# An encoder block on one core: the first pass's loads through one queue, and its side work over more ticks

## The chip, the cores and the metric

The kernel runs on one core of one Trainium2 chip. The metric is the device time of one execution in microseconds (us), lower is better. The kernel before the change takes 3470.04 us (median of 3 runs, 3468.87 to 3470.82).

## The reference

512 tokens of width 2048 in float32 go through one block. What matters here:

```python
h = rms_norm(x, norm1_g);  proj = h @ w_in           # 2048 x 8200: q, k, v, forget logits, pool input, gates
q, k = rms_norm over each head's 128 columns         # 8 heads
attn = softmax(q k' / sqrt(128) + (c_q - c_k), causal) v      # c = cumsum(log_sigmoid(forget logits))
y_attn = attn @ w_branch_attn;  y_pool = multiscale_pool(pin) @ w_branch_pool
x = x + (sig(g_A)*y_attn + sig(g_B)*y_pool) @ w_out
xn = rms_norm(x, norm2_g);  query = xn @ peer_w_query
# per token and head: top 16 of 128 scores twice, top 16 of their 256 sums, softmax,
# then 16 rows of expert_u and of expert_v (16384 x 2048 each)
x = x + sum over heads and picks of gelu(u . xn) * gate * v
```

## The kernel before

The tokens are split in three. The first 128 ("A") go through a **first pass** of their own (about 0 to 436 us); their expert rows are then gathered one by one beside the later passes. The other 384 ("B") go through the same projections in a second run over the weights, and 320 of them meet all experts as dense products. The change touches the first pass alone.

**Weights.** The first pass reads 112 weight tiles of 128 x 2048 float32 (1 MB each): 64 of `w1A` (16 groups of 512 columns, four tiles per group), then 16 each of `wbrA`, `woA` and `wquA`. SP issues every tile's load, in order, as soon as a raw buffer is free (`ensure_load`, L148): three `wraw` buffers and, until the last group of `wbrA`, one `xraw`. Of `w1A`, `wbrA` and `woA` every third tile is used raw, as float32; the other two of three are split in two halves: ScalarE rounds a half to `whi` (L162), VectorE forms the rest, `wlo` (L174). Of `wquA` two of three are raw. A raw buffer is free again when TensorE has read the raw tile, or when `wlo` of the second half is done.

**TensorE's tile** is `mmA` (L240): four steps of K = 128 into 128 x 512 of PSUM, one matmul per step for a raw tile and three for a split one.

**Order.** All engines take their instructions in program order, and the program is written as a schedule by hand. Side work stands in Python generators. In the middle of each weight tile (`kk == 1`) one **tick** runs: every live generator emits what it has up to its next `yield`. `next_w` (L186) emits splits for the tile at hand and the next before the tile's matmuls, `ahead` (L194) emits one more `whi` after them, `after` (L198) the matching `wlo`. `run_gens_last` runs a new generator's first piece at once, between `ahead` and `after`.

**What is touched, in the order of time:**
- Start (L275 to L282): `xA` (the A tokens, transposed, four pieces of 256 KB) and `xr0` (the same tokens as rows, 1 MB) are issued by ScalarE, the first three weight tiles by SP. Then, for each of four pieces (L349 to L352): VectorE multiplies by `g1`, ScalarE rounds, VectorE subtracts; the first weight tile's split stands behind the first piece. Behind all four stands L358, ScalarE's sum of squares of `xr0`, which gives `rsn`, the rows' norm (`narrow_rstd`, emitted in the first tile). `wpg` (1 MB, needed by the pooling generators) is issued by ScalarE at L364.
- Head norms (`qkA_norm`, L475): per group of q or k one eviction (L383), four sums of squares (L480), one Ln and one Exp on ScalarE between VectorE's steps (L482, L321 to L325), a multiply, and three ticks later the transposes. `attendA` (L498) waits five ticks from the v group's end, then uses them; its four `ck` rows (L505) are issued by SP.
- Rows of the other tokens (`rest_rstd`, L545): three 1 MB loads `row<-x` by SP, beside the weights.
- Second inputs (`inputs_b`, L642): sixteen K steps of the B tokens, loaded in pairs by POOL (`xB`, eight loads of 384 KB, two buffers), each multiplied by VectorE (L656), rounded by ScalarE (L658), and its rest formed by VectorE (L662) one or two ticks later.
- Second norm of A (`normedA`, L672), and the scores with top-k (`scores_a`, L866; `job`, L725).

Of the kernel before, what the change touches and what calls it, by code (L numbers as in the profile page):

```python
# [12 lines left out]
F32 = mybir.dt.float32  # L13
# [4 lines left out]
AF = mybir.ActivationFunctionType  # L18
OP = mybir.AluOpType
# [43 lines left out]
def block_kernel(ctx, tc, a):  # L63
# [211 lines left out]
    g1 = const.tile([P, KD], F32, name="g1")  # L275
    nc.gpsimd.dma_start(g1, a["g1"])
    for c in range(4):
        nc.scalar.dma_start(xA[:, 4 * c:4 * c + 4, :].rearrange("p k t -> p (k t)"),
                            a["xA"][:, 4 * c * NA:4 * (c + 1) * NA])
    ensure_load(0)  # L280
    nc.scalar.dma_start(xr0, a["x"][0:P])
    ensure_load(2)  # L282
    jp = const.tile([P, P], I32, name="jp")
    nc.gpsimd.iota(jp, pattern=[[1, P]], base=0, channel_multiplier=-1)
    iot = const.tile([P, P], F32, name="iot")
# [69 lines left out]
            ensure_split(1)  # L355
    nc.vector.tensor_scalar(qg, qg, float(np.float32(P ** -0.5)), None, op0=OP.mult)
    sq0 = row_tile()
    nc.scalar.activation(sq0, xr0, AF.Square, accum_out=ssn[:, 0:1])  # L358
    zA = pz.tile([P, 2 * D], F32, name="zA")
    ap32 = pz.tile([P, KD, NA], F32, name="ap32")  # L360
    aph = pA.tile([P, KD, NA], F32R, name="YH")
    apl = pA.tile([P, KD, NA], F32R, name="YL")
    wpgA = p1.tile([P, D], F32, name="wpg")
    nc.scalar.dma_start(wpgA, a["wpg"])  # L364

    bands = p1.tile([P, 4, P], F32, name="bands")
    bt = p1.tile([P, P], F32, name="bt")
# [106 lines left out]

    def qkA_norm(which, hb, ps):  # L475
        t = rowsA(ps, "raw", 3)
        v = p1.tile([P, 12], F32, name="hv", bufs=2)
        sq = p1.tile([P, S], F32, name="sqA")
        for j in range(4):
            nc.scalar.activation(sq[:, j * P:(j + 1) * P], t[:, j * P:(j + 1) * P], AF.Square,  # L480
                                 accum_out=v[:, j:j + 1])
        nc.vector.tensor_scalar(v[:, :4], v[:, :4], 1.0 / P, EPS, op0=OP.mult, op1=OP.add)  # L482
        rsqrt_nr(v[:, 4:8], v[:, :4], v[:, 8:])
        yield
        nc.vector.tensor_tensor(quad(t), quad(t), v[:, 4:8, None].to_broadcast([P, 4, P]), op=OP.mult)
        for _ in range(3):
            yield
        pt = bank()
        for j in range(4):
            nc.tensor.transpose(pt[:, j * P:(j + 1) * P], t[:, j * P:(j + 1) * P], ident)  # L490
        out = p1.tile([P, 4, NA], F32, name="n%d" % which)
        nc.scalar.activation(out.rearrange("p j t -> p (j t)"), pt, AF.Copy,
                             scale=(kg if which else qg)[:, 0:1])
        qkA[which, hb] = out
        if which:
            nc.scalar.dma_start(kA_d[hb], out)

    def attendA(hb, ps):  # L498
        vA = p1.tile([P, 4, P], F32, name="vA")
        nc.scalar.activation(vA.rearrange("p j t -> p (j t)"), ps, AF.Copy, scale=rsn[:, 0:1])  # L500
        nc.scalar.dma_start(vA_d[hb], vA)
        ck = p1.tile([P, 4, NA], F32, name="ck")
        for j in range(4):
            h = 4 * hb + j
            nc.sync.dma_start(ck[:, j, :], c_d[h:h + 1, :NA].to_broadcast([P, NA]))  # L505
        for _ in range(5):
            yield
        qn, kn = qkA.pop((0, hb)), qkA.pop((1, hb))
        pss = bank()
        for j in range(4):  # L510
            nc.tensor.matmul(pss[:, j * P:(j + 1) * P], lhsT=qn[:, j, :], rhs=kn[:, j, :],
                             start=True, stop=True)
        pr = p1.tile([P, 4, NA], F32, name="prA")
        sm = p1.tile([P, 4, 2], F32, name="smA", bufs=2)
        for j in range(4):
            h = 4 * hb + j
            nc.vector.scalar_tensor_tensor(pr[:, j, :], ck[:, j, :], cT[:, 0, h:h + 1],
                                           pss[:, j * P:(j + 1) * P], op0=OP.subtract, op1=OP.subtract)
        nc.vector.tensor_tensor(pr, pr, mask[:, None, :].to_broadcast([P, 4, NA]), op=OP.add)
        nc.vector.tensor_reduce(sm[:, :, 0:1], pr, axis=AX.X, op=OP.min)  # L520
        yield
        for j in range(4):
            nc.scalar.activation(pr[:, j, :], pr[:, j, :], AF.Exp, bias=sm[:, j, 0:1], scale=-1.0,
                                 accum_out=sm[:, j, 1:2])
        yield
        nc.vector.reciprocal(sm[:, :, 1:2], sm[:, :, 1:2])
        nc.vector.tensor_tensor(pr, pr, sm[:, :, 1:2].to_broadcast([P, 4, NA]), op=OP.mult)
        yield
        yield
        yield  # L530
        pt = bank()
        for j in range(4):
            nc.tensor.transpose(pt[:, j * P:(j + 1) * P], pr[:, j, :], ident)
        PT = p1.tile([P, 4, NA], F32, name="PT")
        nc.scalar.copy(PT.rearrange("p j t -> p (j t)"), pt)
        yield
        yield
        pa = bank()
        for j in range(4):
            nc.tensor.matmul(pa[:, j * P:(j + 1) * P], lhsT=vA[:, j, :], rhs=PT[:, j, :],  # L540
                             start=True, stop=True)
        nc.scalar.copy(ap32[:, 4 * hb:4 * hb + 4, :].rearrange("p j t -> p (j t)"), pa)
        split_to(ap32, aph, apl, 4 * hb)
# [14 lines left out]
    for n, (kind, i) in enumerate(groups_a):  # L558
        ps = acc_bank()
        for q in range(4):  # L560
            mmA(ps, xA, hAh, hAl, 4 * q, q == 0, q == 3, run_gens)
            if n == 0 and q == 0:
                narrow_rstd(0, 1)
            ahead()
            if q < 3:
                after()
        if kind == "pin":
            gens.append(poolA(i, ps))
            if i == 1:
# [72 lines left out]
    def inputs_b():  # L642
        rb = row_bcast(p2, [rsn[:, b:b + 1] for b in range(1, NTB)], "rstdB")
        xs = {}

        def load(c):
            xs[c] = p2.tile([P, 2, NB], F32, name="xB", bufs=2)
            nc.gpsimd.dma_start(xs[c].rearrange("p j t -> p (j t)"), a["xB"][c])

        load(0)  # L650
        for c in range(KD // 2):
            if c + 1 < KD // 2:
                load(c + 1)
            for j in range(2):
                k = 2 * c + j
                nc.vector.scalar_tensor_tensor(xs[c][:, j, :], xs[c][:, j, :], g1[:, k:k + 1], rb,  # L656
                                               op0=OP.mult, op1=OP.mult)
                nc.scalar.copy(hh[:, k, :], xs[c][:, j, :])  # L658
                yield
                if j:  # L660
                    yield
                nc.vector.tensor_tensor(hl[:, k, :], xs[c][:, j, :], hh[:, k, :].bitcast(F32),  # L662
                                        op=OP.subtract)

    gens.append(inputs_b())
    nAh = pA.tile([P, KD, NA], F32R, name="YH")
# [5 lines left out]
    def normedA(i):  # L672
# [5 lines left out]
        for j in range(4):  # L678
            nc.tensor.transpose(tb[:, j * P:(j + 1) * P], xs[:, j * P:(j + 1) * P], ident)
        nc.vector.tensor_tensor(n32[:, 4 * i:4 * i + 4, :], quad(tb),  # L680
                                g2[:, 4 * i:4 * i + 4, None].to_broadcast([P, 4, NA]), op=OP.mult)
        split_to(n32, nAh, nAl, 4 * i)
        yield
        t = p3.tile([P, S], F32, name="scr", bufs=2)
# [181 lines left out]
    def scores_a(c, ps, kk):  # L866
# [18 lines left out]
        scored.append(c)  # L885
        for j in range(2):
            yield from blkA.job(2 * c + j, (s[:, 2 * j, :], s[:, 2 * j + 1, :]))
        chosen.append(c)

    scored, chosen = [], []  # L890
# [706 lines left out]
```

## Time and profile before

| | |
|---|---|
| median of 3 runs | 3470.04 us |
| the profiled execution | 3467.64 us, its span 3465.8 us |
| TensorE matmul busy | 3334.0 us, 96% |
| VectorE / ScalarE / GpSimd busy | 2685.1 us (77%) / 1515.4 us (44%) / 652.4 us (19%) |
| HBM | 980.05 MB read, 53.56 MB written, 298 GB/s over the span |

Engines: PE is TensorE's matmul, PEld its weight load, DVE VectorE, ACT ScalarE, POOL GpSimd, SP SyncE; ACTq, SPq and POOLq are their sequencers, which issue DMAs. Times in the rows are microseconds from the span's start; busy time is the union of an engine's instructions in a stretch. A wait is named by what ended it: `PE psm L240 <- DVE wlo L174` means that the matmul of line 240 began when VectorE's instruction of line 174, which writes `wlo`, had ended. "PEclk" is the clock that TensorE was granted, as a share of 2.4 GHz; 0.50 is 1.2 GHz.

### The profile page before, as it was taken

The page shows a single profiled execution, that of the slowest core. Times are in us where ns is not written, and L with a number is a line of the kernel's source. Part 1 is how long each engine was busy: PE and PEld are TensorE (multiplying, and loading weights), DVE is VectorE, ACT ScalarE, POOL GpSimd, SP SyncE. Part 2 cuts the span into 40 slices and gives each one's busy share as a digit, 9 for nine tenths or more (in the row PEclk, how much of TensorE's full clock was granted, in tenths as well). Part 3 has the DMA queues.
Part 4 walks back from the last instruction along what each step waited for, and adds up shares of the span by engine and source line. Part 5 has one row for each costly group of instructions (what it writes and reads, how often), then busy time and mean ns, then how long its engine had stood idle before and what let it go on. Part 6 is the DMA issues. An engine that isn't in the chain of part 4 may idle for free.

```text
span 3465.8 us, 50471 instructions
## 1 busy us (share of the span) xinstructions
PE 3334.0 (96%) x20236; PEld 3155.4 (91%) x20236; DVE 2685.1 (77%) x3482; ACT 1515.4 (44%) x2263; POOL 652.4 (19%) x411
## 2 busy tenths in 40 slices
PE   7999899999998999999999989999999999999998
PEld 5656599999998999999999989999999999999997
DVE  5556787787876876887778758888887888888885
ACT  5655434545443333346476753333333333333332
POOL 0000012233321221310000002222222222222221
PEclk9999999999998999999999999999999999999999
DMA  7898867787877897864555689999998999899994
GB/s 263 305 360 313 312 239 272 268 312 268 309 288 283 319 362 278 312 229 161 201 189 193 215 305 345 357 355 351 350 347 338 359 354 354 338 358 353 340 357 151
DMA packets 226762, 1036.90 MB, mean 299 GB/s; under 512 B 21344, under 2 KB 107536, under 8 KB 112928
## 3 DMA queue, kind: packets, MB, share of 16 engines
q1 hardware_dynamic: 144640, 574.14, 44.4%
q0 software_dynamic: 56480, 406.96, 31.5%
q10 hardware_dynamic: 25408, 52.59, 3.9%
q8 instruction: 158, 2.59, 0.3%
q14 instruction: 76, 0.62, 0.0%
HBM read 980.05 MB, written 53.56 MB: 298 GB/s over the span
## 4 chain that ended last, share of the span: by engine, by line
PE 55%; DVE 14%; issue 12%; DMA 8%; ACT 7%; POOL 2%; ACTq 0%; SPq 0%; POOLq 0%; DVEq 0%
PE psm L223 9%; PE psm L221 9%; PE psm L222 9%; PE psv L222 6%; PE psv L223 6%; PE psv L221 6%; PE psm L240 6%; DVE wlo L174 5%; DMA row<-v,gidx 3%; ACT whi L162 3%; ACT o L1385 2%; DVE tok L827 1%; POOL row L787 1%; PE psx L222 1%; PE psx L223 1%
## 5 line engine op out<-in xcount | busy, mean ns | idle before, releaser
L174 DVE TENSOR_TENSOR wlo<-wraw,whi 128x1024 fp32r<-128x1024 f32 x728 | 869.2, 1220 | 294.9 <-ACT whi L162 291.6
L162 ACT CAST whi<-wraw 128x1024 fp32r<-128x1024 f32 x728 | 753.5, 1047 | 658.0 <-PE psv L222 375.9
L223 PE MATMUL psv<-h5h,wlo 128*128 128x320 f32 x2048 | 636.1, 311 | 14.3 <-DVE wlo L174 14.3
L221 PE MATMUL psm<-xnh,whi 128*128 128x320 f32 x2048 | 637.4, 311 | 10.3 <-ACT at L1410 9.8
L221 PE MATMUL psv<-h5h,whi 128*128 128x320 f32 x2048 | 636.7, 311 | 6.6 <-ACT h5h L1442 6.4
L223 PE MATMUL psm<-xnh,wlo 128*128 128x320 f32 x2048 | 634.3, 310 | 6.7 <-DVE wlo L174 6.6
L222 PE MATMUL psv<-h5l,whi 128*128 128x320 f32 x2048 | 637.4, 311 | 1.1
L222 PE MATMUL psm<-xnl,whi 128*128 128x320 f32 x2048 | 633.8, 309 | 0.0
L787 POOL DMA_INDIRECT row<-v,gidx x139 | 219.1, 1576 | 1136.4 <-DVE tok L827 1090.1
L223 PEld LDWEIGHTS psv<-h5h,wlo 128*128 128x128 f32 x2048 | 386.9, 189 | 15.3 <-DVE wlo L174 15.3
L221 PEld LDWEIGHTS psm<-xnh,whi 128*128 128x128 f32 x2048 | 386.5, 189 | 10.8 <-ACT at L1410 10.0
L221 PEld LDWEIGHTS psv<-h5h,whi 128*128 128x128 f32 x2048 | 387.0, 189 | 8.8 <-ACT h5h L1442 8.8
L223 PEld LDWEIGHTS psm<-xnh,wlo 128*128 128x128 f32 x2048 | 386.3, 189 | 8.1 <-DVE wlo L174 8.1
L222 PEld LDWEIGHTS psv<-h5l,whi 128*128 128x128 f32 x2048 | 386.9, 189 | 4.9 <-DVE h5l L1443 4.6
L222 PEld LDWEIGHTS psm<-xnl,whi 128*128 128x128 f32 x2048 | 386.5, 189 | 0.0
L221 PE MATMUL psm<-hh,whi 128*128 128x384 f32 x1024 | 353.6, 345 | 0.0
L787 POOL DMA_INDIRECT row<-u,gidx x135 | 223.8, 1658 | 660.1 <-DVE row L824 567.2
L222 PE MATMUL psm<-hl,whi 128*128 128x384 f32 x1024 | 346.4, 338 | 0.0
L223 PE MATMUL psm<-hh,wlo 128*128 128x384 f32 x1024 | 346.4, 338 | 0.0
L827 DVE SCALAR_TENSOR_TENSOR tok<-row,gact,tok 128x2048 f32<-128x2048 f32 x139 | 326.0, 2345 | 19.1 <-DMA row<-v,gidx 18.0
L824 DVE SCALAR_TENSOR_TENSOR row<-row,tok 128x2048 f32<-128x2048 f32 x135 | 307.4, 2284 | 9.1 <-DMA row<-u,gidx 9.0
L162 ACT CAST whi<-xraw 128x1024 fp32r<-128x1024 f32 x148 | 153.5, 1046 | 182.2 <-PE psv L222 145.7
(393 smaller groups left out, 5183.4 us busy)
## 6 DMA issues: line engine op xcount, KB each, us to landing
wraw<-uT SPq DMA_DIRECT2D x112, 1024.0 KB, 6.7
wraw<-vd SPq DMA_DIRECT2D x96, 1024.0 KB, 7.4
wraw<-w1A SPq DMA_DIRECT2D x48, 1024.0 KB, 6.7
xraw<-vd SPq DMA_DIRECT2D x32, 1024.0 KB, 9.4
wraw<-wgl SPq DMA_DIRECT2D x23, 1024.0 KB, 8.4
g_d<-stg ACTq DMA_DIRECT2D x10, 2048.0 KB, 10.9
gt<-g_d SPq DMA_DIRECT2D x32, 640.0 KB, 10.3
xraw<-w1A SPq DMA_DIRECT2D x16, 1024.0 KB, 7.3
```

The costliest lines, as they stand in the source:

```text
L162: nc.scalar.copy(hi, raws[i][:, half * HD:(half + 1) * HD])
L174: nc.vector.tensor_tensor(lo, raws[i][:, half * HD:(half + 1) * HD], hi.bitcast(F32), op=OP.subtract)
L221: nc.tensor.matmul(ps, lhsT=wh, rhs=xh, start=first and i == 0, stop=False)
L222: nc.tensor.matmul(ps, lhsT=wh, rhs=xl, start=False, stop=False)
L223: nc.tensor.matmul(ps, lhsT=wl, rhs=xh, start=False, stop=last and i == n - 1)
L240: nc.tensor.matmul(ps, lhsT=xs[:, k, :], rhs=ws, start=first and kk == 0 and n == 0, stop=last and kk == 3 and n == len(terms) - 1)
L787: nc.gpsimd.indirect_dma_start(out=r, out_offset=None, in_=a[kind], in_offset=bass.IndirectOffsetOnAxis(ap=gidx[grp][:, j:j + 1], axis=0))
L824: nc.vector.scalar_tensor_tensor(r, r, 1.0, tok, op0=OP.mult, op1=OP.mult, accum_out=gact[:, j:j + 1])
L827: nc.vector.scalar_tensor_tensor(tok, r, gact[:, j:j + 1], tok, op0=OP.mult, op1=OP.add)
L1385: nc.scalar.activation(o2[:, j, :], o2[:, j, :], AF.Copy, scale=idT[2][:, 4 * q + j:4 * q + j + 1])
```

## The change

- `xA`'s four pieces, the first weight tile after the first piece, the next two weight tiles, then `xr0`, all issued by SP in this order. `wpg` is issued by SP in the second group's first tile.
- The sum of squares of `xr0` moves from ahead of the first tile to behind the second; `narrow_rstd` from the first to the third.
- `qkA_norm`: two more yields, so that eviction, squares, and Ln/Exp stand in three ticks.
- `ck` is issued by POOL.
- `inputs_b`: multiply, rounding and rest of one K step stand in three successive ticks; two pairs are loaded at the start, and a further pair when the rest of its buffer's last user is formed.
- `normedA` (three of four) and `scores_a`: one more yield each.

```diff
--- before.py
+++ after.py
@@ -275,11 +275,12 @@
     g1 = const.tile([P, KD], F32, name="g1")
     nc.gpsimd.dma_start(g1, a["g1"])
     for c in range(4):
-        nc.scalar.dma_start(xA[:, 4 * c:4 * c + 4, :].rearrange("p k t -> p (k t)"),
-                            a["xA"][:, 4 * c * NA:4 * (c + 1) * NA])
-    ensure_load(0)
-    nc.scalar.dma_start(xr0, a["x"][0:P])
+        nc.sync.dma_start(xA[:, 4 * c:4 * c + 4, :].rearrange("p k t -> p (k t)"),
+                          a["xA"][:, 4 * c * NA:4 * (c + 1) * NA])
+        if c == 0:
+            ensure_load(0)
     ensure_load(2)
+    nc.sync.dma_start(xr0, a["x"][0:P])
     jp = const.tile([P, P], I32, name="jp")
     nc.gpsimd.iota(jp, pattern=[[1, P]], base=0, channel_multiplier=-1)
     iot = const.tile([P, P], F32, name="iot")
@@ -355,13 +356,11 @@
             ensure_split(1)
     nc.vector.tensor_scalar(qg, qg, float(np.float32(P ** -0.5)), None, op0=OP.mult)
     sq0 = row_tile()
-    nc.scalar.activation(sq0, xr0, AF.Square, accum_out=ssn[:, 0:1])
     zA = pz.tile([P, 2 * D], F32, name="zA")
     ap32 = pz.tile([P, KD, NA], F32, name="ap32")
     aph = pA.tile([P, KD, NA], F32R, name="YH")
     apl = pA.tile([P, KD, NA], F32R, name="YL")
     wpgA = p1.tile([P, D], F32, name="wpg")
-    nc.scalar.dma_start(wpgA, a["wpg"])
 
     bands = p1.tile([P, 4, P], F32, name="bands")
     bt = p1.tile([P, P], F32, name="bt")
@@ -474,11 +473,13 @@
 
     def qkA_norm(which, hb, ps):
         t = rowsA(ps, "raw", 3)
+        yield
         v = p1.tile([P, 12], F32, name="hv", bufs=2)
         sq = p1.tile([P, S], F32, name="sqA")
         for j in range(4):
             nc.scalar.activation(sq[:, j * P:(j + 1) * P], t[:, j * P:(j + 1) * P], AF.Square,
                                  accum_out=v[:, j:j + 1])
+        yield
         nc.vector.tensor_scalar(v[:, :4], v[:, :4], 1.0 / P, EPS, op0=OP.mult, op1=OP.add)
         rsqrt_nr(v[:, 4:8], v[:, :4], v[:, 8:])
         yield
@@ -502,7 +503,7 @@
         ck = p1.tile([P, 4, NA], F32, name="ck")
         for j in range(4):
             h = 4 * hb + j
-            nc.sync.dma_start(ck[:, j, :], c_d[h:h + 1, :NA].to_broadcast([P, NA]))
+            nc.gpsimd.dma_start(ck[:, j, :], c_d[h:h + 1, :NA].to_broadcast([P, NA]))
         for _ in range(5):
             yield
         qn, kn = qkA.pop((0, hb)), qkA.pop((1, hb))
@@ -559,11 +560,15 @@
         ps = acc_bank()
         for q in range(4):
             mmA(ps, xA, hAh, hAl, 4 * q, q == 0, q == 3, run_gens)
-            if n == 0 and q == 0:
-                narrow_rstd(0, 1)
             ahead()
             if q < 3:
                 after()
+            if n == 0 and q == 1:
+                nc.scalar.activation(sq0, xr0, AF.Square, accum_out=ssn[:, 0:1])
+            elif n == 0 and q == 2:
+                narrow_rstd(0, 1)
+            elif n == 1 and q == 0:
+                nc.sync.dma_start(wpgA, a["wpg"])
         if kind == "pin":
             gens.append(poolA(i, ps))
             if i == 1:
@@ -647,20 +652,28 @@
             xs[c] = p2.tile([P, 2, NB], F32, name="xB", bufs=2)
             nc.gpsimd.dma_start(xs[c].rearrange("p j t -> p (j t)"), a["xB"][c])
 
+        def high(k):
+            nc.scalar.copy(hh[:, k, :], xs[k // 2][:, k % 2, :])
+
+        def low(k):
+            nc.vector.tensor_tensor(hl[:, k, :], xs[k // 2][:, k % 2, :], hh[:, k, :].bitcast(F32),
+                                    op=OP.subtract)
+
         load(0)
-        for c in range(KD // 2):
-            if c + 1 < KD // 2:
-                load(c + 1)
-            for j in range(2):
-                k = 2 * c + j
-                nc.vector.scalar_tensor_tensor(xs[c][:, j, :], xs[c][:, j, :], g1[:, k:k + 1], rb,
-                                               op0=OP.mult, op1=OP.mult)
-                nc.scalar.copy(hh[:, k, :], xs[c][:, j, :])
+        load(1)
+        for k in range(KD + 2):
+            if 0 < k <= KD:
+                high(k - 1)
+            if k > 1:
+                low(k - 2)
+                if k % 2 and k // 2 + 1 < KD // 2:
+                    load(k // 2 + 1)
+            if k < KD:
+                nc.vector.scalar_tensor_tensor(xs[k // 2][:, k % 2, :], xs[k // 2][:, k % 2, :],
+                                               g1[:, k:k + 1], rb, op0=OP.mult, op1=OP.mult)
+            yield
+            if k % 2:
                 yield
-                if j:
-                    yield
-                nc.vector.tensor_tensor(hl[:, k, :], xs[c][:, j, :], hh[:, k, :].bitcast(F32),
-                                        op=OP.subtract)
 
     gens.append(inputs_b())
     nAh = pA.tile([P, KD, NA], F32R, name="YH")
@@ -679,6 +692,8 @@
             nc.tensor.transpose(tb[:, j * P:(j + 1) * P], xs[:, j * P:(j + 1) * P], ident)
         nc.vector.tensor_tensor(n32[:, 4 * i:4 * i + 4, :], quad(tb),
                                 g2[:, 4 * i:4 * i + 4, None].to_broadcast([P, 4, NA]), op=OP.mult)
+        if i < 3:
+            yield
         split_to(n32, nAh, nAl, 4 * i)
         yield
         t = p3.tile([P, S], F32, name="scr", bufs=2)
@@ -885,6 +900,8 @@
         scored.append(c)
         for j in range(2):
             yield from blkA.job(2 * c + j, (s[:, 2 * j, :], s[:, 2 * j + 1, :]))
+            if j == 0:
+                yield
         chosen.append(c)
 
     scored, chosen = [], []
```

## Rows read from the trace of the kernel before

**Rows 1.** The page's first part, whole span: busy us (share) xinstructions.

```profile
PE 3334.0 (96%) x20236; PEld 3155.4 (91%) x20236; DVE 2685.1 (77%) x3482; ACT 1515.4 (44%) x2263; POOL 652.4 (19%) x411
```

**Rows 2.** Busy time by stretch: start:end us, length, engines, PEclk, DMA share, GB/s.

```profile
10.28:15.70 5.42, 5.38 (x12) 3.49 (x12) 4.32 (x5) 1.78 (x3) 0.00 (x0) 1.00 1.01 411
15.70:25.80 10.10, 0.01 (x2) 0.01 (x1) 2.16 (x5) 3.96 (x6) 0.00 (x0) 0.64 0.78 303
25.80:32.08 6.28, 6.24 (x13) 4.30 (x14) 4.01 (x10) 5.39 (x7) 0.00 (x0) 0.50 0.64 232
...
93.68:100.35 6.67, 4.11 (x11) 3.27 (x12) 5.80 (x9) 5.11 (x8) 0.00 (x0) 0.74 0.74 242
...
148.16:154.96 6.80, 4.20 (x11) 3.30 (x12) 5.88 (x9) 5.29 (x7) 0.00 (x0) 0.75 0.81 306
...
180.81:208.72 27.91, 21.90 (x76) 13.05 (x77) 14.28 (x18) 14.42 (x23) 0.00 (x0) 1.00 0.99 394
208.72:305.00 96.28, 96.04 (x358) 64.91 (x357) 58.15 (x61) 56.93 (x68) 0.00 (x0) 1.00 0.87 327
...
330.00:376.00 46.00, 42.16 (x145) 25.09 (x144) 31.20 (x41) 21.37 (x31) 2.86 (x5) 1.00 0.87 330
...
395.00:404.13 9.13, 4.81 (x11) 2.63 (x11) 8.92 (x32) 3.47 (x5) 0.00 (x0) 0.63 0.71 268
...
438.27:600.00 161.73, 161.42 (x892) 151.57 (x891) 133.02 (x207) 61.71 (x95) 34.09 (x18) 1.00 0.66 245
```

**Rows 3.** TensorE's waits in 0 to 455 us: total us, times, longest.

```profile
PE psm L240 <- ACT whi L162: 23.3, 7, 10.3
PE psm L240 <- DVE wlo L174: 10.1, 12, 2.6
PE psx L874 <- ACT scr L868: 8.3, 2, 4.3
PE psm L240 <- DMA wraw<-w1A: 3.4, 1, 3.4
```

**Rows 4.** Timeline of the start: start us, us, instruction, [idle before <-releaser].

```profile
7.50 0.69 DVE L349 TENSOR_TENSOR xA<-xA,g 128x512 f32<-128x512 f32 x1 [4.14 <-DMA g<-g]
...
17.89 0.69 DVE L349 TENSOR_TENSOR xA<-xA,g 128x512 f32<-128x512 f32 x1 [1.12 <-DMA xA<-xA]
18.61 0.62 ACT L351 CAST XH<-xA 128x512 fp32r<-128x512 f32 x1 [2.57 <-DVE xA L349]
...
22.81 1.91 ACT L358 ACTIVATE row<-xr 128x2048 f32<-128x2048 f32 x1 [3.58 <-DMA xr<-x]
...
24.71 1.97 ACT L162 CAST whi<-wraw 128x1024 fp32r<-128x1024 f32 x2
```

**Rows 5.** DMA issues in 0 to 0.9 us: count, KB each, us to landing.

```profile
wraw<-w1A SPq DMA_DIRECT2D x1, 1024.0 KB, 6.3
xA<-xA ACTq DMA_DIRECT2D x1, 256.0 KB, 6.5
```

**Rows 6.** Timeline around the first k group's norm.

```profile
88.47 1.05 ACT L162 CAST whi<-wraw 128x1024 fp32r<-128x1024 f32 x1 [2.49 <-DMA wraw<-w1A]
...
91.45 0.17 DVE L482 TENSOR_SCALAR hv<-hv 128x4 f32<-128x4 f32 x1 [5.04 <-ACT sqA L480]
...
94.48 0.16 DVE L323 SCALAR_TENSOR_TENSOR hv<-hv 128x4 f32<-128x4 f32 x1 [2.87 <-ACT hv L322]
...
94.96 2.36 DVE L174 TENSOR_TENSOR wlo<-wraw,whi 128x1024 fp32r<-128x1024 f32 x2
```

**Rows 7.** Waits of SP's queue in 168 to 182 us: total us, times, longest.

```profile
SPq L152 <- DMA kA_d<-n: 6.8, 1, 6.8
```

**Rows 8.** The tile xB in 300 to 430 us: ns min/median/max; waits; landings.

```profile
L656 DVE SCALAR_TENSOR_TENSOR xB<-xB,g,rstdB x16: 606/610/617, 319.1 to 404.8; 128x384 f32<-128x384 f32 x16
...
ACT hh L658: 33.8, 16
...
DMA to landing us min/median/max: 5.3/7.1/8.4
```

## The prediction

> **What bounds the kernel now.** I read the page's busy times first, then a table of stretches of the first pass, then TensorE's waits, then the timeline around each wait.
>
> TensorE is busy 96% of the span [rows 1], so what can be won is the idle 4% and the time at half clock. The change touches the first 436 us only. Behind them TensorE is busy 161.42 of 161.73 us at full clock [rows 2]: there TensorE itself sets the pace, its program is the same, and an earlier start should be carried to the end. So the sum is made of the first pass's holes.
>
> The table of stretches shows them [rows 2]. In 208.72 to 305 TensorE never stops, with the DMA engines at 0.87: the weights' supply keeps up when nothing disturbs it. The holes are: 10.10 us at 15.70, then 6.28 us at half clock; 2.56 us at 93.68 and 2.60 at 148.16 (6.67 less 4.11, 6.80 less 4.20); 6.0 us between 180.81 and 208.72; 3.8 between 330 and 376; 4.3 at 395. By the waits [rows 3] the releaser is mostly `whi` or `wlo`, the split of a weight half: ScalarE and VectorE are late with it, though neither is near full.
>
> A hole costs more than itself. The clock in 93.68 to 100.35 is 0.74, in 148.16 to 154.96 0.75 [rows 2]: 0.26 x 6.67 and 0.25 x 6.80 us of clock, 1.7 us each, after a wait of 2.6.
>
> **The start.** The second tile's `whi` starts at 24.71, because ScalarE stood at the sum of squares at 22.81, which waited for `xr0` to land [rows 4]. `whi` itself needs only its weight and ScalarE, and ScalarE's last rounding of `xA` ends at 18.61 + 0.62 = 19.23. With the squares behind the second tile, `whi` starts 24.71 - 19.23 = 5.5 us earlier. Then `xA`: VectorE waited 1.12 us for the fourth piece at 17.89 [rows 4]. At 411 GB/s [rows 2] 1 MB takes 2.55 us. In one queue the first piece and the first weight are 1.25 MB, landed at about 7.1 as now (0.75 + 6.3 [rows 5]); pieces two to four follow in 1.9 us, near 9.0, and the 1.1 us goes. The second and third weight land near 11.6 and 14.1, before 18.1, when they are wanted. The first multiply waits at 7.50 for `g1` [rows 4], which POOL issues before and after; with one big queue beside it instead of two it may land sooner, at most until the first weight's 7.1 binds: the first tile's `whi` stands behind that multiply and the rounding, 7.50 + 0.69 + 0.62 = 8.8, so 0 to 1.7 us. I take 0.9. Sum 5.5 + 1.1 + 0.9 = 7.5; ends 5.5 (the squares alone) and 8.3. Half clock after the restart costs 6.28 x 0.5 = 3.1 us now; the gap shrinks from 10.1 to some 3 us, and the holes of 2.6 still cost 1.7, so 0 to 1.4 more, taken as 0.
>
> What is late next: the squares (1.9 us, [rows 4]) and the Ln/Exp pair (about 3 us, 91.45 to 94.48 in [rows 6]) now lie beside tiles two to four, whose halves must be made then too. The first reader of the norm is the eviction after tile four, at least three tiles later; the cover is that each half is emitted a tile ahead. Without it, 3 us. `wpg` comes through SP between two weights and puts every later load back by 2.55 us once; the pooling matmuls need it three tiles later, and the next tiles' loads have had a queue at 232 GB/s of 411 [rows 2]. I cost it at 0, end 2.55.
>
> At this place the Trainium skill (DMA: Bandwidth & Descriptors, Issuing engines are not separate DMA queues) speaks against the new queue: DMAs of all issuers run on the same 16 engines, and issuing from several saves only the issue time. By it the single queue is worth nothing by itself and the start gives the squares' 5.5 us alone. The row shows more: a 256 KB piece took 6.5 us and the 1 MB weight beside it 6.3 [rows 5], so the two queues advance in step and each piece waits for a weight, which one queue's order undoes.
>
> **Head norms.** After the first k group `whi` is ready at 88.47 + 1.05 = 89.5, but its `wlo` starts only at 94.96 [rows 6]: VectorE stands first at L482 (5.04 us idle, for the squares), then at L323 (2.87 us, for Ln and Exp), and `wlo` is queued behind them since the norm is emitted between `ahead` and `after`. TensorE wants it at 93.68. After the change only the eviction is emitted there, and `wlo` runs at 89.5 to 90.7, 3 us early. The squares follow a tick later; the lump of Ln/Exp another tick later holds ScalarE and VectorE 3 us as now, but in mid-tile, behind the splits of the next two tiles. The second q group does the same at 148.16. Each hole is worth 2.6 + 1.7 = 4.3: together 8.6, taken 8.5. Low end 0 (the lump makes the same hole where it now stands). The two tick later transposes are still before `attendA` uses them.
>
> **ck through POOL.** 6.0 us are lost in 180.81 to 208.72, 3.4 of them at once on a weight's landing [rows 2, 3]. That weight was late because SP stood 6.8 us before it until a store, `kA_d`, had landed [rows 7], a tile that it doesn't read: I read it as a completion mark that the two share in turn. Four `ck` between them go to POOL, and the store moves two ticks later, so the turn no longer falls so; SP loads about 4 us earlier. POOL has little else then (19% in all [rows 1]); `ck` is due five ticks after its issue. The three `row<-x` stay in SP's queue and the DMA engines are at 0.99 [rows 2], so I take 4.5 of 6.0; ends -1 and 6.
>
> **Second inputs, second norm.** ScalarE's rounding waited 33.8 us in 16 waits for VectorE's multiply of the same tick [rows 8], and `whi` behind it came late: 3.8 us of TensorE in 330 to 376. In three ticks these waits go. But a new one comes: a pair's load is now issued two ticks before its multiply, not three. A K step takes (404.8 - 319.1) / 15 = 5.7 us, and is 1.5 ticks, so two ticks are 7.6 us now, and some 6.2 without the holes. The landing takes 5.3 to 8.4 [rows 8]. So six multiplies may wait up to 2.2 us each, and VectorE's next `wlo` behind them, where now ScalarE's sixteen waits of 2.1 us cost 3.8. I take a gain of 2.5; ends 3.8, and a loss of 6 x 2.2 = 13.
>
> **Top-k.** One job's ten instructions (2 to 3 us of VectorE) move a tick later: 0. The 4.3 us at 395 come from a score's eviction that ScalarE has behind a `whi` [rows 3]; with 0.37 x 9.13 = 3.4 of clock [rows 2] they are worth 7.7. I leave them, end 7.7.
>
> **Sum.** 7.5 + 8.5 + 4.5 + 2.5 = 23.0 us. The profiled execution took 3467.6 us with a span of 3465.8; 23.0 off gives 3444.6. The runs' median is 2.4 above it, so 3447.
>
> **The rivals.**
> - *The eviction's hole closes too* (395): 7.7 more, 3439. For it: VectorE has less in one tick. Against: its `whi` waits for a load. 0.12.
> - *Given back in the first pass.* The start's 7.5 and part of the norms come, but a TensorE without holes eats the weights as they land, and waits of the same size appear at loads: 10 us in all, 3460. For it: 0.99 of DMA at 180 to 208. Against: 96 us without a hole at 0.87. 0.17.
> - *Nothing that shows.* SP's queue takes over `xA`, `xr0` and `wpg`, 3 MB at 2.55: 7.6 us later weights; if supply binds from there, that cancels the start, and the norms' holes move instead of closing: 3463 to 3475. Against: the same bytes ran on the same engines before. 0.10.
> - *Slower: the loads of the second inputs.* All six multiplies wait 2.2 us, each wait reaches TensorE and takes the clock with it (1.7): 6 x 3.9 = 23; with the scores' loads behind them late as well, twice that, 47 less the 23 won: 3494. It decides from the point where a landing is beyond the two ticks and VectorE has no slack; it has some 30% (31.20 of 46 us busy [rows 2]). 0.05.
>
> **How the numbers follow.** The forecast has 0.56, by its own terms 3440 to 3455. The range must hold most of the first two rivals: 3436 to 3463. About 0.2% (6.9 us) is what a measurement can tell from no change. Faster by more: 0.56 + 0.12 + 0.17 = 0.85; within: 0.10; slower: 0.05.
>
> **What would show it.** Right: the second tile's `whi` at 16 to 18.5 us, ahead of the squares; no wait over 1 us at the k and q norms; no SP wait on `kA_d`; ScalarE's waits before L658's rounding gone; the end of the first pass (about 436 now) near 413. Wrong: VectorE's multiply of `xB` waiting for a DMA, with TensorE waits behind it; a wait of 2 us or more on `wlo` a tick or two after a norm; the same span behind the first pass not kept.

## The result, and the profile after

The changed kernel takes 3447.27 us (median of 4 runs, 3444.61 to 3449.02), the kernel before 3469.56 beside it (4 runs, 3468.87 to 3470.82): ratio 0.9935, 95% interval 0.9921 to 0.9949. The profiled execution took 3449.02 us, its span 3447.0: 18.6 us less than the one of before, where the sum forecast 23.0. The places below are read from one profiled execution of each kernel. Seven of these kernels have the same program up to tile 80 of the first pass, and there they stand 19.7 to 22.7 us ahead of the kernel before: a difference of 1 us between two traces means nothing.

The page's first part, against [rows 1]: the same work, 19 us less around it.

```profile
PE 3335.7 (97%) x20236; PEld 3156.8 (92%) x20236; DVE 2686.0 (78%) x3482; ACT 1513.1 (44%) x2263; POOL 645.6 (19%) x419
```

To see where the time came from, the first matmul of each of the 112 weight tiles was read off both timelines (tiles are counted from 0, so the second is tile 1; "before" is the time in the kernel before). How much earlier each comes after the change:

| point | before, us | earlier by, us |
|---|---|---|
| second weight tile | 25.80 | 8.2 |
| tile 16, ahead of the k norm | 86.49 | 8.5 |
| tile 19, behind the k norm | 100.12 | 12.3 |
| tile 35, behind the second q norm | 154.54 | 16.7 |
| tile 44, behind the late weight of 181 to 209 | 187.34 | 20.4 |
| tiles 48 to 80 | 202.64 to 302.36 | 21.2 to 21.4 |
| tile 82 | 310.05 | 22.3 |
| tile 84, behind `inputs_b`'s first piece | 320.60 | 19.5 |
| tile 91 | 346.23 | 22.5 |
| tile 99 | 374.09 | 18.75 |
| first matmul of the B tokens | 435.8 | 18.4 |
| B tokens, behind the top-k's last pieces | 496 | 12.2 |
| B tokens, near the end of the second pass | 1196 | 11.3 |
| dense products, first experts | 1530 to 2049 | 7.4 |
| dense products | 2990 | 13.9 |
| dense products | 3080 | 19.5 |
| end of the span | 3465.8 | 18.8 |

So 21.3 us come in the first 300 us and 2.9 go again in the next 130. The 3030 us behind the first pass keep the rest as a sum only: 11.0 of it are lost by 2049 and 11.4 won back later. Stretches of after (columns as in [rows 2]):

```profile
14.55:17.57 3.02, 0.00 (x2) 0.00 (x1) 2.07 (x5) 1.66 (x4) 0.00 (x0) 0.97 1.02 426
17.57:20.82 3.25, 3.21 (x7) 2.11 (x8) 2.90 (x5) 1.32 (x2) 0.00 (x0) 0.50 1.03 429
75.00:100.00 25.00, 25.00 (x99) 17.42 (x99) 14.15 (x19) 17.43 (x29) 0.00 (x0) 1.00 0.89 343
135.00:150.00 15.00, 15.00 (x57) 10.05 (x56) 8.15 (x11) 10.26 (x21) 0.00 (x0) 1.00 0.81 326
172.00:200.00 28.00, 26.50 (x101) 17.34 (x100) 15.64 (x22) 20.56 (x33) 0.00 (x0) 1.00 0.94 376
292.00:298.00 6.00, 2.29 (x8) 1.17 (x6) 3.15 (x6) 1.99 (x2) 0.00 (x0) 0.94 0.70 283
310.00:358.00 48.00, 42.82 (x147) 25.65 (x146) 31.57 (x42) 21.61 (x33) 2.89 (x5) 1.00 0.93 332
...
465.90:475.00 9.10, 5.76 (x12) 3.94 (x13) 7.52 (x11) 1.64 (x3) 1.91 (x2) 0.62 0.25 77
```

The gap of 10.10 us at the start is 3.02; the stretches of the k and q norms have no hole and full clock (25.00 of 25.00, 15.00 of 15.00); of the 6.0 us in [rows 2]'s 180.81 to 208.72, 1.5 are left in 172 to 200. But 292 to 298 now has TensorE busy for 2.29 of 6.00, and 310 to 358 loses 5.2 where 330 to 376 lost 3.8; the last line is taken up at the top-k below. (292 to 298 lies ahead of tile 84; 310 to 358 holds tiles 87 to 99.)

TensorE's waits in 0 to 436, against [rows 3]:

```profile
PE psm L240 <- ACT whi L162: 14.6, 6, 9.0
PE psx L889 <- ACT scr L883: 8.5, 2, 4.6
PE psm L240 <- DVE wlo L174: 5.2, 9, 1.1
PE psx L340 <- DVE dg L339: 3.7, 1, 3.7
```

The waits on `whi` and `wlo` fell from 33.4 to 19.8, the one on a weight's landing is gone. The last line is the hole at 295 (in before 2.1 at most): a broadcast of three row norms, whose diagonal tiles `dg` VectorE makes behind a weight's two `wlo`. That weight's `whi` had itself waited for the landing; ScalarE's and VectorE's rows:

```profile
293.52 1.99 ACT L162 CAST whi<-wraw 128x1024 fp32r<-128x1024 f32 x2 [1.85 <-DMA wraw<-woA]
...
294.60 2.36 DVE L174 TENSOR_TENSOR wlo<-wraw,whi 128x1024 fp32r<-128x1024 f32 x2 [2.21 <-ACT whi L162]
296.88 0.47 DVE L339 TENSOR_SCALAR dg<-ident,rsn 128x128 f32<-128x128 f32 x2
```

The start, against [rows 4]. The second tile's `whi` runs at 16.48, right behind the last rounding of `xA`; no multiply waits for a piece behind the first. The first multiply comes 0.82 us earlier.

```profile
6.68 0.69 DVE L350 TENSOR_TENSOR xA<-xA,g 128x512 f32<-128x512 f32 x1 [3.31 <-DMA g<-g]
...
15.95 0.62 ACT L352 CAST XH<-xA 128x512 fp32r<-128x512 f32 x1 [1.36 <-DVE xA L350]
16.48 1.99 ACT L162 CAST whi<-wraw 128x1024 fp32r<-128x1024 f32 x2
```

The k norm, against [rows 6]. `wlo` is formed right behind its `whi` (there it stood 5 us behind); Ln and Exp still hold VectorE for 3.13 us ahead of 90.73 (2.56 of it two table loads of 1.28 us on ScalarE), but the `wlo` of the tiles at hand are made before.

```profile
80.39 1.05 ACT L162 CAST whi<-wraw 128x1024 fp32r<-128x1024 f32 x1 [2.36 <-DMA wraw<-w1A]
...
81.48 1.23 DVE L174 TENSOR_TENSOR wlo<-wraw,whi 128x1024 fp32r<-128x1024 f32 x1 [1.39 <-ACT whi L162]
...
85.17 2.36 DVE L174 TENSOR_TENSOR wlo<-xraw,whi 128x1024 fp32r<-128x1024 f32 x2 [0.94 <-ACT whi L162]
87.44 0.16 DVE L483 TENSOR_SCALAR hv<-hv 128x4 f32<-128x4 f32 x1
90.73 0.16 DVE L324 SCALAR_TENSOR_TENSOR hv<-hv 128x4 f32<-128x4 f32 x1 [3.13 <-ACT hv L323]
```

SP no longer waits for `kA_d` in 140 to 200 [rows 7], and of the 33.8 us for which ScalarE waited at the second inputs' rounding [rows 8] 2.9 are left.

### The profile page after: what moved, and what is told of

It reads as the page before. It is cut to its first block, busy times and chain, and to the rows that moved or that the text cites. A ratio compares the mean times of both kernels' runs of the same rounds, so it can differ in the third digit from the quotient of the medians.

```text
span 3447.0 us, 50487 instructions
## 1 busy us (share of the span) xinstructions
PE 3335.7 (97%) x20236; PEld 3156.8 (92%) x20236; DVE 2686.0 (78%) x3482; ACT 1513.1 (44%) x2263; POOL 645.6 (19%) x419
## 4 chain that ended last, share of the span: by engine, by line
PE 46%; issue 25%; DVE 9%; DMA 5%; ACT 4%; POOL 2%; ACTq 0%; POOLq 0%; SPq 0%; DVEq 0%
PE psm L223 7%; PE psm L222 7%; PE psm L221 7%; PE psv L222 6%; PE psv L223 6%; PE psv L221 6%; DVE wlo L174 3%; DVE tok L842 2%; DMA row<-v,gidx 2%; POOL row L802 2%; PE psm L240 1%; PE psx L222 1%; PE psx L223 1%; PE psx L221 1%; ACT whi L162 1%
## 5 line engine op out<-in xcount | busy, mean ns | idle before, releaser
L223 PEld LDWEIGHTS psm<-xnh,wlo 128*128 128x128 f32 x2048 | 387.3, 189 | 13.9 <-DVE wlo L174 13.9
L223 PEld LDWEIGHTS psv<-h5h,wlo 128*128 128x128 f32 x2048 | 386.1, 189 | 12.2 <-DVE wlo L174 12.2
L802 POOL DMA_INDIRECT row<-u,gidx x136 | 215.1, 1582 | 679.8 <-DVE row L839 513.0
```

What stands on the lines that cost most here:

```text
L223: nc.tensor.matmul(ps, lhsT=wl, rhs=xh, start=False, stop=last and i == n - 1)
L802: nc.gpsimd.indirect_dma_start(out=r, out_offset=None, in_=a[kind], in_offset=bass.IndirectOffsetOnAxis(ap=gidx[grp][:, j:j + 1], axis=0))
```

## The experiments

"Ends" is the first matmul of the B tokens in the profiled execution: 435.8 before, 417.4 after. Ratios are against the kernel before, with 95% intervals. e1 to e4 put one part of the change alone into the kernel before, e8 and e9 half a part; in the others a part is taken out of the changed kernel, or something is added to it.

**e1_start_alone.** The start only: the queue's order, the squares behind the second tile, `wpg`.

```diff
-        nc.scalar.dma_start(xA[:, 4 * c:4 * c + 4, :].rearrange("p k t -> p (k t)"),
+        nc.sync.dma_start(xA[:, 4 * c:4 * c + 4, :].rearrange("p k t -> p (k t)"),
...
-    nc.scalar.activation(sq0, xr0, AF.Square, accum_out=ssn[:, 0:1])
+            if n == 0 and q == 1:
+                nc.scalar.activation(sq0, xr0, AF.Square, accum_out=ssn[:, 0:1])
```

> The kernel before with the start's part alone (xA, first weights, xr0 and wpg through SP's queue, the squares behind the second tile, the norm behind the third). Theory: the first pass's holes add up, and this part's gain is carried to the end: the second tile of TensorE starts near 17.6 us instead of 25.8, and the kernel is 8 us faster (range 6.5 to 9.5). Rival, given back: the earlier start meets late loads before 93 us; the shift is below 4 us there and at the end.

3459.68 us, 0.9972 (0.9961 to 0.9984). The second tile starts 7.2 us earlier; 7.5 are left at the end of the first pass (428.3), and the span is 7.9 shorter: the theory holds.

**e2_norms_alone.** The two yields of `qkA_norm` only.

```diff
         t = rowsA(ps, "raw", 3)
+        yield
...
+        yield
         nc.vector.tensor_scalar(v[:, :4], v[:, :4], 1.0 / P, EPS, op0=OP.mult, op1=OP.add)
```

> The kernel before with the two yields in the head norms alone. Theory: the holes of 2.6 us behind the first k and the second q group close, each with 1.7 us of half clock: 8.6 us faster (7 to 10). The hole at 181 to 209 us: if ck's four transfers through SP set the turn of the completion marks, it stays within 1.5 us of its 6.0; the rival is that the store kA_d, which comes two ticks later here too, closes it alone, and then the gain is 12 to 13 us.

3455.13 us, 0.996 (0.9948 to 0.9972); ends 425.8, 10.0 earlier. 4.3 come at each of the two norms, and 4.4 more at 181 to 209, the hole that was booked to `ck`: the rival, that the store's later place closes it alone, holds. The hole at `dg`, then, 4.3 us long, gives 3.2 back.

**e3_ck_alone.** `ck` through POOL only.

```diff
-            nc.sync.dma_start(ck[:, j, :], c_d[h:h + 1, :NA].to_broadcast([P, NA]))
+            nc.gpsimd.dma_start(ck[:, j, :], c_d[h:h + 1, :NA].to_broadcast([P, NA]))
```

> The kernel before with ck issued by POOL alone. Theory: the four ck transfers set the turn by which a weight load waits for the store kA_d; without them SP does not wait for it, the hole at 181 to 209 us shrinks from 6.0 to 1.5, and the kernel is 4.5 us faster (3 to 6). Rival: the store's place decides, and ck alone changes nothing (0, within 1.5).

3462.04 us, 0.9976 (0.9967 to 0.9986); ends 431.9, 3.9 earlier: 4.55 come at that same hole, and the hole at `dg` (4.0 us) gives part back. Another 2.1 came before, at the second q norm, where TensorE waited 2.1 us (2.6 before) and, in this execution, the clock did not fall behind the wait. SP's waits around it, e2 and then e3 (total us, times, longest):

```profile
SPq L152 <- PE psm L240: 30.0, 6, 6.0
...
SPq L152 <- DMA wraw<-w1A: 3.2, 2, 1.7
```

```profile
SPq L152 <- PE psm L240: 28.0, 5, 7.2
...
SPq L152 <- DMA kA_d<-n: 0.4, 1, 0.4
```

Either edit takes the wait of 6.8 us away: e2 moves the store, e3 the four loads that stood between. In the whole change the two win the 4.4 once. Why SP waited for that store at all, the shared completion mark of the prediction, no run shows directly.

**e4_inputs_alone.** The spread of the second inputs and the yield of `normedA` only.

```diff
+        load(1)
+        for k in range(KD + 2):
+            if 0 < k <= KD:
+                high(k - 1)
+            if k > 1:
+                low(k - 2)
...
-                nc.scalar.copy(hh[:, k, :], xs[c][:, j, :])
```

> The kernel before with inputs_b in three ticks and normedA's yield alone. Theory after the result: the stretch 305 to 376 us is bound by the weights' loads with three raw buffers, so ScalarE's waits on VectorE (33.8 us before L658) turn into waits on weight loads, and TensorE gains nothing: 0 to 3 us slower. Rival, the prediction's step: 2.5 us faster (1.5 to 4). Second rival: VectorE waits for xB loads, 6 waits of 1 to 2 us, and that is what costs.

3466.95 us, 0.9996 (0.9987 to 1.0004): no difference; ends 437.8, 2.1 later, of which 1.3 stand there by tile 82, ahead of the part's first instruction. The interval (4.5 us faster to 1.4 slower) does not exclude the 2.5 of the rival by itself; the first pass, where the rival would have to show, does not have it. ScalarE's waits, before (300 to 436) and then e4 (305 to 440):

```profile
ACT hh L658 <- DVE xB L656: 33.8, 16, 3.5
ACT whi L162 <- DMA wraw<-wquA: 13.0, 5, 5.5
ACT whi L162 <- DMA wraw<-woA: 7.5, 4, 5.5
```

```profile
ACT whi L162 <- DMA wraw<-woA: 23.2, 9, 5.4
ACT whi L162 <- DMA wraw<-wquA: 19.0, 6, 6.8
...
ACT hh L651 <- DVE xB L667: 3.5, 3, 1.5
```

The 33.8 us became 3.5, as the change says, and the waits for weights to land went from 20.5 to 42.2. So ScalarE had for the most part waited for VectorE while the next weight was still on its way: the wait was cover, not cost.

**e5_no_inputs.** The changed kernel with this part undone (the diff of e4 backwards).

> The changed kernel with inputs_b and normedA as before. Theory: in 294 to 420 us the changed kernel lost 2.8 us of the 21.3 won by then, because of this part; so without it the shift stays at 20 to 21.5 us to the end of the first pass, and the kernel is 20 to 24 us faster than before (2 to 3 faster than the changed one). Rival: an earlier first pass loses those 2.8 us in any case (start alone and head norms alone lost 0.4 to 1 there), and this part is worth 0 within 1.

3448.14 us, 0.9937 (0.9924 to 0.9951); ends 416.7 where the whole change ends 417.4. The gain of 2 to 3 us that the theory expected of undoing it fell; within the whole change, too, the part is worth nothing. From tile 82 to the end of the first pass the changed kernel loses 3.9 us and this one 3.0, so most of that loss is not its doing.

**e6_raw4, e7_raw4_no_inputs.** If late weights are the limit there, a fourth raw buffer must make the spread pay. `tok` (1 MB) is not yet used in this stretch; it serves for `woA` and three quarters of `wquA`. e6 is the changed kernel with it, e7 the same without the spread. `Spare` hands `tok`'s buffer to `ensure_load`; with it set, loads are also issued three tiles ahead instead of two, so the two things come together.

```diff
+    extra["raws"] = Spare(prow)
...
     for i in range(4):
+        if i == 3:
+            extra["raws"] = None
```

> The changed kernel with a fourth raw weight buffer in the stretch of woA and the first three groups of wquA (the buffer of tok, which is idle then). Theory: this stretch is bound by loads that wait for one of three raw buffers; ScalarE's waits on weight loads there (38 us on woA and wquA) fall by half or more, TensorE's holes of 0.3 to 1.2 us go, and the first pass ends 3 to 8 us earlier than in the changed kernel. Rival: the DMA engines are the limit (0.87 busy); the waits stay and the time is the same within 1.5 us.

> The fourth raw buffer with inputs_b and normedA as before, the rest as changed. Theory: with loads no longer late, the spread of inputs_b shows its worth: this kernel is 1.5 to 4 us slower than the fourth buffer with the spread, ScalarE waiting some 30 us on VectorE's multiply of xB. Rival: the spread is worth nothing with four buffers either (within 1).

e6: 3445.49 us, 0.9932 (0.9918 to 0.9945), ends 408.1. e7: 3450.78 us, 0.9947 (0.9933 to 0.996), ends 418.4. ScalarE's waits in 280 to 420, e6 and then e7:

```profile
ACT whi L171 <- DMA wraw<-wquA: 10.9, 4, 3.8
ACT whi L171 <- DMA wraw<-woA: 9.8, 6, 5.2
ACT hh L666 <- DVE xB L682: 7.5, 5, 2.1
```

```profile
ACT hh L673 <- DVE xB L671: 24.8, 15, 3.5
ACT whi L171 <- DMA wraw<-woA: 9.6, 5, 4.2
```

TensorE's in e7:

```profile
PE psx L888 <- ACT scr L882: 8.8, 2, 5.5
PE psx L349 <- DVE dg L348: 7.5, 1, 7.5
```

Counted from tile 82, ahead of the second inputs, to the end of the first pass: with three buffers the spread is worth -0.9 us, with four 9.1; without the spread the fourth buffer wins nothing (-0.5). It took both to win. Of the 9.1, 2.7 come at `dg` (a wait of 7.5 us in e7, 4.8 in e6) and 5.2 at the first score's eviction, which in e7 stands behind a `whi` that waited 4.1 us for its weight. No wait of TensorE in e7 ends with the second inputs' rounding, so that ScalarE's 24.8 us of waits are what makes e7 late is not shown. These are single executions; the medians of e6 and e7 lie 5.3 us apart, with intervals that overlap a little. Of e6's 9.3 us of first pass against the changed kernel the span shows 3.8 and the median 1.8; these two kernels' intervals overlap too.

**e8_queue_only, e9_square_only.** The start in its two halves, each in the kernel before: the queue's order with the squares in place, and the squares moved with the queues as they were; one line of the first edit, then the second's.

```diff
+        nc.sync.dma_start(xA[:, 4 * c:4 * c + 4, :].rearrange("p k t -> p (k t)"),
```

```diff
+            if n == 0 and q == 1:
+                nc.scalar.activation(sq0, xr0, AF.Square, accum_out=ssn[:, 0:1])
```

> The kernel before with xA, first weights and xr0 through SP's queue, but the squares where they were. Theory: xr0 lands near 17 us instead of 22.8, the squares run behind the last rounding of xA (near 17 to 19) and delay the second tile by their 1.9 us alone: its matmuls start near 20 us, 5 to 6 us faster. Rival by the rule that all issuers share the 16 engines, so that the queue does not matter: xr0 lands near 22 and nothing is won (within 1).

> The kernel before with the squares behind the second tile and the norm behind the third, the queues as before. Theory: the second tile's weight half is ready behind the last rounding of xA, so TensorE's second tile starts 5.5 us earlier, at 20.3 us; with the late-load places of the queue's run alone (181 to 209 us and 294 to 302 us) 1 to 5 us of it are left at the end of the first pass. Rival: it is carried whole, 5 to 6 us.

e8: 3464.72 us, 0.9989 (0.998 to 0.9998). e9: 3462.23 us, 0.998 (0.9971 to 0.9989). Their second tiles start 5.0 and 5.7 us earlier, against 7.2 for both in e1. ScalarE in e8 and then in e9 (start, us, instruction):

```profile
17.77 1.91 ACT L359 ACTIVATE row<-xr 128x2048 f32<-128x2048 f32 x1 [1.13 <-DMA xr<-x]
...
19.68 1.98 ACT L162 CAST whi<-wraw 128x1024 fp32r<-128x1024 f32 x2
```

```profile
18.46 0.62 ACT L351 CAST XH<-xA 128x512 fp32r<-128x512 f32 x1 [2.55 <-DVE xA L349]
...
18.99 1.99 ACT L162 CAST whi<-wraw 128x1024 fp32r<-128x1024 f32 x2
```

In e8 all of `xA` and `xr0` land earlier, so the squares stand 5 us earlier too. At the end of the first pass e9 keeps 4.8 us (431.0) and e8 0.9 (434.9): of e8's 5.0, 3.0 go at the late weight of 181 to 209, 3.0 at `dg`, and some 2 come in between.

**e10_dg_split, e11_scr_first, e12_best.** What is left, attacked: the changed kernel with the diagonal tiles made a tick ahead of their matmuls (e10), with the score's eviction ahead of the next splits (e11), and with both and the fourth buffer (e12).

```diff
+            nc.vector.tensor_scalar(dgs[-1], ident, rsn[:, b:b + 1], None, op0=OP.mult)
+        yield
...
+            if q == 3:
+                gens.append(scores_a(i, ps, kk))
+                run_gens_last()
             ahead()
             after()
-        gens.append(scores_a(i, ps, kk))
-        run_gens_last()
```

> The changed kernel with the three diagonal tiles of row_bcast made by VectorE one tick ahead of the matmuls that read them. Theory: TensorE's wait of 3.7 us at 293 us (1.7 of clock behind it) comes from the matmul's place right behind VectorE's instruction, which has a late weight's split ahead of it; with a tick between, it falls below 1 us and the first pass ends 3 to 5.5 us earlier. Rival: the late weight itself binds there; the wait moves to the weight's matmul and nothing is won (within 1).

> The changed kernel with each score's eviction ahead of the next weights' splits on ScalarE. Theory: the waits at 376 us (4.6 us and 3.4 of clock) and at 410 us (3.9 and 3.4) end when the eviction need not wait for a weight's landing: 6 to 11 us faster than the changed kernel. Rival: the splits come late instead, TensorE waits for whi, and nothing is won (within 1.5).

> The changed kernel with all three: a fourth raw buffer in the stretch of woA and wquA, the diagonal tiles a tick ahead, the score's eviction ahead of the splits. Theory: the holes are separate, the first pass ends 14 to 20 us earlier than in the changed kernel, near 400 us, and the kernel is 0.9 to 1.2% faster than before. Rival: they share one cause, the weights' landing, and the three together bring no more than the fourth buffer alone (9 us in the first pass).

e10: 3444.52 us, 0.9931 (0.9917 to 0.9945), ends 405.1, span 3438.9. e11: 3442.89 us, 0.9927 (0.9913 to 0.994), ends 410.9, span 3440.8. e12: 3452.12 us, 0.9952 (0.9939 to 0.9966), ends 420.6. TensorE's waits in 280 to 420, e11 and then e12 (to 425):

```profile
PE psx L340 <- DVE dg L339: 3.9, 1, 3.9
...
PE psx L895 <- ACT scr L891: 2.0, 1, 2.0
PE psx L889 <- ACT scr L883: 1.0, 1, 1.0
```

```profile
PE psm L249 <- ACT YH L426: 5.5, 1, 5.5
PE psm L249 <- DVE wlo L183: 5.3, 3, 2.8
...
PE psx L665 <- DVE dg L661: 3.7, 1, 3.7
```

e10 has no wait on `dg`, as its theory says, and e11's waits at the score's first reader fell from 8.5 to 1.0 us (those at the second rose from 0.7 to 2.0). They end the first pass 12.3 and 6.5 us earlier than the changed kernel. For e10 that is far more than the 3 to 5.5 expected: 7.4 are there at tile 84, and why the later places keep them and add to them was not followed. For e11 the first pass shows the low end of its 6 to 11; the median does not reach it. As medians they are 2.8 and 4.4 us below the changed kernel, with overlapping intervals: the same, or a little faster. e12 misses its theory: its first pass ends 3.2 us later than the changed kernel's, not 14 to 20 earlier. That is less than the fourth buffer alone brings, which the rival allows but does not explain. Together with the fourth buffer the wait on `dg` is back (VectorE forms two `wlo` of a weight that could be split earlier ahead of it, as at 295 in the changed kernel), and a new one of 5.5 comes on `YH`. Why the three together end the first pass 15.5 us behind e10 is not settled beyond these waits. No version beats the changed kernel clearly.

## Why the prediction was right, and where it was not

The forecast of 3447.0 met 3447.27, but by less than it looks. Its sum was wrong by 4.4 us (3444.6 against 3449.02 profiled); the profiled execution of before lay 2.4 below its median and that of after 1.8 above, which made up for it by luck. Of the signs that it named, the split at 16.48, the norms, `kA_d` and the second inputs' waits came as said; the end of the first pass did not (417.4, not 413). By steps:

- **Start**, 7.5 forecast: 8.2 measured at the second tile, 7.2 in e1, where 7.5 are kept. The mechanism is as argued. The clock's share, "0 to 1.4" taken as 0, is right as a sum: in the changed kernel's profiled execution the restart ran at half clock for 3.25 us instead of 6.28 [rows 2], and a later stretch at half clock from 48.1 on (6.83 us, 3.41 before) took that back (the gain is 9.7 us at tile 8 and 8.0 at tile 10). The shorter gap is not the reason for the 3.25: e5, with a gap of 3.23 us at the same place, restarts at half clock for 6.20, and e1, with 3.4, for 5.90. The squares were worth 5.7 alone (5.5 forecast), but the two halves are not additive: 5.0 and 5.7 make 7.2. The 0.9 taken for `g1` came in the changed kernel (0.82), but in e1 TensorE's first tile starts only 0.2 us earlier.
- **The rule weighed there** (Trainium skill, DMA: Bandwidth & Descriptors, Issuing engines are not separate DMA queues): by it the one queue is worth nothing. e8 shows 5.0 us at the second tile, so the rule misses what the order in a queue does to the time of landing; it was nearly right for the kernel as a whole, where 0.9 us of first pass is left (0.9989 of the time, 0.998 to 0.9998).
- **Head norms**, 8.5: 4.3 and 4.3 measured, in the change and in e2, each 2.6 of wait and 1.7 of clock. The mechanism is as argued.
- **`ck` through POOL**, 4.5: 4.4 measured. The size was right; the cause only in half. The later store closes the hole without `ck` being moved (e2), and `ck` closes it without the store (e3), so in the whole change that line of the diff wins nothing of its own that these runs show.
- **Second inputs, second norm**, 2.5: the step that failed. It read ScalarE's 33.8 us of waits as the cause of 3.8 us of TensorE's. They went, as said, and nothing was won: -0.8 us of first pass alone (e4) and -0.9 in the change, both within the scatter of the traces. The price it feared did not come either: the multiplies wait for `xB`'s landing 2.1 us in 2 cases, not 13. In place of those waits stand waits for weights to land. That the three raw buffers set the limit is likely and not shown: with four, and loads three tiles ahead, the same edit goes with 9.1 us of first pass, but 7.9 of them at `dg` and at the score's eviction.
- **Given back**: a rival at 0.17 with 10 us; in the first pass it came with 2.9. The table shows two losses: 2.8 us at the `dg` broadcast (tiles 82 to 84), which are back at tile 91, and 3.7 between tiles 91 and 99, which are not; there TensorE waits 4.7 us for `wlo`, `whi` and weights, where before it waited 2.5. The prediction never named the `dg` broadcast. Its hole grows from 2.1 us to between 4.0 and 4.7 in e2, e3, e8 and e9 as well (e1: 2.6). In the changed kernel VectorE serves it behind a `wlo` pair of a weight that lands late; how much TensorE loses there does not follow from how early it comes (e1 is 7.7 us early and waits 2.6, e8 is 3.1 early and waits 4.1). Without it (e10) the first pass ends 12.3 us earlier.
- **Top-k**, 0: wrong as a mechanism. The piece that moves is not hidden. In 440 to 480 TensorE now waits where it did not before:

```profile
PE psx L982 <- DVE mx L973: 3.4, 1, 3.4
```

The wait ends with VectorE's `mx`, queued behind the decoding of picks (`sel` is its last step):

```profile
466.89 1.22 DVE L771 TENSOR_REDUCE sel<-eq 128x64 f32<-128x1024 bf16 x1
...
468.62 0.56 DVE L973 SCALAR_TENSOR_TENSOR mx<-sc 128x384 f32<-128x384 f32 x1
```

The clock is 0.62 in 465.90 to 475.00, so that some 6.8 us are lost.
- **Behind the first pass**, the span kept: right as a sum (3030.1 and 3029.6), and that is luck. The prediction took 162 us without a hole [rows 2] for all 3030. In fact the gain of 18.4 us is 12.2 at 496, 7.4 from 1530 to 2049, and 19.5 at 3080. The last dense phase is 9.4 us shorter (1370.4 to 1360.9), with fewer waits; TensorE's there, before and then after:

```profile
PE psv L223 <- DVE wlo L174: 14.3, 4, 7.9
PE psv L221 <- ACT h5h L1442: 6.4, 4, 2.7
```

```profile
PE psv L223 <- DVE wlo L174: 11.1, 3, 7.6
PE psv L221 <- ACT h5h L1459: 2.4, 2, 2.2
```

All seven kernels with the yield in `scores_a` have this shape: they lose 11 to 16 us between the first matmul of the B tokens and 2049, and win 10 to 12 from there to the end; their second pass (to the first matmul of `wo` for the B tokens) takes 781 to 785 us. The six changed ones without it lose 3.4 at most and win 3.9 at most, and their second pass takes 775, as in the kernel before. One trace of the way there: the gather of A's first expert row starts 55 to 56 us behind the first matmul of the B tokens with the yield and 46 without, so the work on the 384 gathered rows falls beside other weight tiles. As sums the seven take 3029.6 to 3035.1 us behind the first pass, the seven without it 3027.3 to 3030.1. So this yield may cost a few us. It was not run alone, and its part in this stays open.
- **The eviction's hole**: it stayed, two waits of 8.5 us in all, as the forecast had it. It was the next thing to win in the first pass (e11: 6.5).

## What to carry to other kernels

A wait of one engine on another that is long and regular is not worth its length: see first what the waiting engine will stand at next, and if that is a load, look at the buffers before moving instructions. A hole closed early in a chain with a fixed supply is to be followed to the next places where a side instruction stands behind bulk work that waits for a load, for there a part is given back. A gain is not carried to the end by itself: follow it from stage to stage, for a sum that comes out can hide a loss of 11 us and a win of the same size. Where two edits touch the same wait, run each alone before booking the gain to either.

## What the runs showed of the hardware that was not expected

With two queues side by side the first piece of 256 KB took 6.5 us [rows 5]; ScalarE's first wait on it ended at 7.36 us, with one queue in the order of use at 3.97. The second tile came 5.0 us earlier by the order alone (e8), though the DMA engines moved little more (426 GB/s in 14.55 to 17.57 of the changed kernel, 411 in 10.28 to 15.70 before).

The length of TensorE's gap did not tell how long it then ran at 1.2 GHz: after 10.10 us it was 6.28, after 3.02 us 3.25, after 3.23 us (e5) 6.20, after the new wait of 3.35 us at 466 it was 5.5. After the waits of 2.6 us at the norms the clock fell for 3.4 us, and after one of 2.1 us in e3, at the second q norm, it stayed at full.
